# Identity product of the last tokens' second column piece moved behind the piece's first matmuls, and two VectorE steps moved behind the extra column

## The chip, the cores and the metric

The kernel runs on one core of a Trainium2 chip. The metric is device time in microseconds from one launch of the whole program; lower is better. Engines are called TensorE (PE in the rows), VectorE (DVE), ScalarE (ACT), GpSimd (POOL) and SyncE (SP). A "q" behind an engine's name marks its instruction queue, which issues transfers (DMAs).

## The reference

One layer of a hybrid encoder block over 512 tokens of width 1024. Only its last lines matter here: the feed-forward part's down projection is added to the residual stream, and each token's row of 1024 numbers is then divided by its root mean square and multiplied by a gain.

```python
def rms_norm(x, g):
    y = x * lax.rsqrt(jnp.mean(x * x, axis=-1, keepdims=True) + EPS)
    return y * g

def conv_glu_ffn(h, w_up, w_conv, b_conv, w_down):
    a, u = jnp.split(h @ w_up, 2, axis=-1)
    return (jax.nn.gelu(dwconv3(a, w_conv, b_conv)) * u) @ w_down

    x = x + merged @ w_out[l]
    x = x + conv_glu_ffn(rms_norm(x, ffn_norm_g[l]), w_ffn_up[l], ...)
return rms_norm(x, final_norm_g)
```

A token's norm needs the sum of squares over its whole row, so nothing of a row can be written out before its last column is known.

## The kernel before

All matrix products run in a split form. Each float32 operand is cut into a high part and a remainder, and one product becomes three matmuls (high x high, high x low, low x high). For the down projection these three are the lines of `tile_mm` (L1256, L1257, L1258). A matmul of 512 columns comes every 0.23 us there, one of 256 columns every 0.12 us.

The down projection is done as seven products of half-size blocks, in the manner of Winograd. The last of them is T4. It has 11 steps over the inner dimension; a step takes 128 rows of weights, which arrive by DMA in pairs (tile `wr`), are cut into `wh` and `wl` by ScalarE and VectorE (L242, L243), and for the last five steps are kept in three larger buffers (`u_8441`, `u_8442`, `u_8443` in the lists below).

The tokens lie in four blocks of 128, the output columns in two halves of 512. `cv(t, f)` is the residual sum, in SBUF, of token block `t` and column half `f`. T4 ends the columns of half 0 for the token blocks 2 and 3; everything else is complete before it. Its sums lie in PSUM:

- block 2, half 0 (`pa_[0]`, `at_6569` in the lists): all 11 steps, 512 columns.
- block 3, half 0 (`pa_[1]`, `at_6570`): the first six steps with 512 columns. The last five (`hold=5`) are held back until block 2 is done, and then run in two pieces of 256 columns (`ends=pieces`): columns `one_` go on in `pa_[1]`, columns `two_` go into another bank, `pl` (`at_8384`).

The residual of block 3 comes in through TensorE, by a product with the identity matrix in float32, which the trace shows as two passes. For the first piece that is `last_residual` (L1419). For the second piece it is `last_half`: VectorE first adds the six finished steps to the residual (L1423), and the identity product (L1424) then opens bank `pl` with that sum.

`product` runs over the pairs of steps. The dictionary `then` names other work that is issued behind a given pair's weights, so entry 3 of T4 stands behind the fourth pair; entries are closures over VectorE, ScalarE and GpSimd steps, among them `finish(t, ...)`, which scales and writes out token blocks 0 and 1. `tc.issue_after(x)` puts what is issued in its body behind instruction `x` in the order of issue. Each engine runs its own list strictly in order, and waits between engines are placed by the framework from the tiles that are read and written; it also keeps reads of one PSUM tile by two engines in their order of issue.

After T4, the tail of the kernel (L1433 to L1457) does the norm of blocks 2 and 3:

- VectorE adds block 2's sum to the residual (L1433), ScalarE squares and sums it (L1272), VectorE adds the other half's sum (L1287), GpSimd raises it to the power -1/2 (L1288, one column), ScalarE and VectorE scale the two halves (L1444, L1294 called from L1446), and SyncE writes the block out (L1447).
- Block 3's first piece is copied with the gain (`oa`, L1436, VectorE) and squared (L1272, ScalarE, straight out of PSUM). Its sum `v` (L1440) goes through a power (L1442, GpSimd) into an extra column of `pl`, which holds the square root of the sum so far (L1449, VectorE). ScalarE squares the second piece together with that column (L1451), so that its sum is the row's whole sum; a last power (L1452) gives the row's factor. ScalarE scales half 1 (L1453) and writes it out (L1454); VectorE scales the second and first pieces (L1455, L1456), and SyncE writes them (L1457).

Of the kernel before, what the change touches and what calls it, by code (L numbers as in the profile page):

```python
# [14 lines left out]
ALU = mybir.AluOpType  # L15
# [4 lines left out]
D = 1024  # L20
# [5 lines left out]
HF = FT // 2  # L26
HB = (HF + 1) // 2
Hf = S // 2
# [93 lines left out]
def hybrid_block(ctx, tc, xg, xT, memT, wflat, vecs, gbias, nabias, out):  # L122
    nc = tc.nc
    V, A, G, PE, SY = nc.vector, nc.scalar, nc.gpsimd, nc.tensor, nc.sync
# [16 lines left out]
    def unit(dt=F32):  # L141
        return up.tile([P, UNIT], dt, tag="unit", name=nm("u"))

    def scr(n=512):
        return sp.tile([P, S], F32, tag="scr", name=nm("s"))[:, :n]

    def tiny(n):
        return tp.tile([P, 32], F32, tag="tiny", name=nm("y"), bufs=12)[:, :n]

    def mmps():  # L150
        return mmp.tile([P, 512], F32, tag="mm", name=nm("mm"))

    def atps():
        return atp.tile([P, 512], F32, tag="at", name=nm("at"))
# [37 lines left out]
    st = {"raw": 0, "split": 0}  # L192
# [55 lines left out]
    def weights(key):  # L248

        i, _, n = BINDEX[key]  # L250
        while st["raw"] <= min(i + RAW_AHEAD, len(BLOCKS) - 1):
            emit_raw(st["raw"])
            st["raw"] += 1
        while st["split"] <= min(i + SPLIT_AHEAD, len(BLOCKS) - 1):
            emit_split(st["split"])
            st["split"] += 1
        return split.pop(i)
# [59 lines left out]
    ident = cp.tile([P, P], F32, name="ident")  # L317
# [132 lines left out]
    def flush():  # L450

        while late:
            late.pop(0)()
# [19 lines left out]
    for k in range(KT):  # L473
        if k % 2 == 0:
            ws = weights(("mlq", k // 2))
# [86 lines left out]
    for c in range(3):  # L562
        n, nk = TMC[c], TMK[c]
        pss = [(mmps if c % 2 else atps)() for _ in range(NT)]
        for h in range(KT // nk):
            ws = weights(("tm", c, h))
# [6 lines left out]
        for t in range(NT):  # L573
# [7 lines left out]
            if c > 0:  # L581
# [5 lines left out]
                for q in range(2):  # L587
                    V.scalar_tensor_tensor(nvv[:, q, 1:3, :], pv[:, q], rc[:, t:t + 1], nvv[:, q, 0:4:3, :].bitcast(F32),
                                           op0=ALU.mult, op1=ALU.subtract)
# [513 lines left out]
    for i in range(4):  # L1103
        ws = weights(("memv", i))
# [10 lines left out]
    for f in range(4):  # L1115
        ps = proj(("naq", f), XH, XL)
        V.tensor_tensor(nq[:, f * S:(f + 1) * S].rearrange("p (b r c) -> p b r c", r=ROWS, b=4), rv(ps), rv(rb),
                        op=ALU.mult)
# [15 lines left out]
    for br in range(3):  # L1134
# [19 lines left out]
        for fp in range(4):  # L1154
# [8 lines left out]
            ws = weights(("br", br, fp))  # L1163
# [49 lines left out]
    def cv(t, f):  # L1213
        o = t % 2 * D + f * S
        return C[t // 2][:, o:o + S]
# [9 lines left out]
    pieces = [("R", 4), ("H", 4), ("nab", 2), ("E", 1)]  # L1225
    r0 = [tp.tile([P, S], F32, tag=tag, name=nm("r"), **({} if n < 4 else {"bufs": 4})) for tag, k in pieces for n in [k] for _ in range(k)]
    one_, two_ = slice(0, Hf), slice(Hf, S)

    def parts():

        us = [unit(F32R) for _ in range(3)]
        at = lambda i: us[i // 8][:, i % 8 * Hf:(i % 8 + 1) * Hf]
        return [at(2 * k) for k in range(HF)], [at(2 * k + 1) for k in range(HF)], us

    def product(name, ab, banks, first, hold=0, then={}, ends=None):

        ah, al, _ = ab
        ws = []
        for i in range(HB):
            ws += weights(("dn", name, i))  # L1240
            if i == 0:
                flush()
            with tc.issue_after(st["lo"]), tc.issue_after(st["hi"]):
                for g in then.get(i, ()):
                    g()
            for k in range(2 * i, len(ws)):
                for t in range(2):
                    if k < HF - hold or t == 0:
                        tile_mm(ah[k], al[k], ws[k], banks[t], t, first and k == 0)
        for bank, c in ends or []:  # L1250
            for k in range(HF - hold, HF):
                tile_mm(ah[k], al[k], [w[:, c] for w in ws[k]], bank, 1, False)

    def tile_mm(ah, al, w, bank, t, start):
        ts = slice(t * P, (t + 1) * P)
        PE.matmul(bank, ah[:, ts], w[0], start=start, stop=False, skip_group_check=True)  # L1256
        PE.matmul(bank, ah[:, ts], w[1], start=False, stop=False, skip_group_check=True)  # L1257
        PE.matmul(bank, al[:, ts], w[0], start=False, stop=True, skip_group_check=True)  # L1258

    def gather(banks, a, f, op):  # L1260

# [5 lines left out]
    ss = [sv[:, 2 * t:2 * t + 2] for t in range(NT)]  # L1267
# [16 lines left out]
    def power(t, v, f):  # L1284

        col = tiny(1)
        V.tensor_tensor(col, ss[t][:, f:f + 1], v, op=ALU.add)  # L1287
        G.tensor_tensor(col, col, nhalf[:, :1], op=ALU.pow)  # L1288
        return col

    def scaled(t, f, col, dst=None):

        dst = cv(t, f) if dst is None else dst
        V.scalar_tensor_tensor(dst, cv(t, f), col, gfin[:, f * S:(f + 1) * S], op0=ALU.mult, op1=ALU.mult)  # L1294

    def finish(t, v):

        col = power(t, v, 1)
        for f in range(2):
            scaled(t, f, col)  # L1300
        SY.dma_start(out[t * P:(t + 1) * P, :], C[t // 2][:, t % 2 * D:(t % 2 + 1) * D])
# [17 lines left out]
    for hh in range(2):  # L1319
# [6 lines left out]
        for j in range(HF):  # L1326
            f = HF * hh + j
            if f == 0:
# [7 lines left out]
                k = KT - 1  # L1336
# [47 lines left out]
        if hh == 0:  # L1384
            pa_, pd = [atps() for _ in range(2)], [mmps() for _ in range(2)]
            product("B11", a11, pa_, True, then={0: [conved], 1: [gelu], 2: [gated]})
            product("T3", s3, pd, True, then={1: [lambda: gather(pa_, 0, 0, ALU.add)]})
            late.append(lambda b=pd: (gather(b, 1, 0, ALU.subtract), gather(b, 1, 1, ALU.add)))
    pd, pc = [mmps() for _ in range(2)], [atps() for _ in range(2)]
    s2, gfin = parts(), unit()  # L1390
    SY.dma_start(gfin[:, :D], gbias[16:].partition_broadcast(P))

    def wide_slices(ab, cols):
# [8 lines left out]
        return [lambda u=u: group(u, min(4, HF - 4 * u)) for u in range(3)]  # L1402

    product("B21", a12, pd, True, then={0: [conved], 1: [gelu], 2: [gated]})
    a22 = parts()
    product("T1", s1, pc, True, then=also(slices(s2, r0, one_, 0), 1, lambda: gather(pd, 0, 0, ALU.add)))
# [6 lines left out]
    vs = {}  # L1413

    pl = atps()
    pieces = ((pa_[1][:, one_], one_), (pl[:, :Hf], two_))
# [2 lines left out]
        PE.matmul(pieces[0][0], ident, cv(3, 0)[:, one_], start=False, stop=False, skip_group_check=True)  # L1419

    def last_half():
        c = cv(3, 0)[:, two_]
        V.tensor_tensor(c, c, pa_[1][:, two_], op=ALU.add)  # L1423
        PE.matmul(pieces[1][0], ident, c, start=True, stop=False, skip_group_check=True)  # L1424

    product("T4", a22, pa_, False, hold=5, ends=pieces, then={
        0: [lambda: vs.update({t: early(t, t // 2) for t in range(NT)})],
        1: [lambda: gather(pc, 0, 1, ALU.add), lambda: ready(1, 0, 1)],
        2: [last_residual, lambda: finish(0, vs[0])],
        3: [last_half, lambda: finish(1, vs[1])],  # L1430
        4: [lambda: V.tensor_tensor(cv(2, 1), cv(2, 1), gfin[:, S:D], op=ALU.mult),
            lambda: V.tensor_tensor(cv(3, 1), cv(3, 1), gfin[:, S:D], op=ALU.mult)]})
    V.tensor_tensor(cv(2, 0), cv(2, 0), pa_[0], op=ALU.add)  # L1433
    squares(cv(2, 0), 2, 0)
    oa, ob = scr(), scr()
    left = V.tensor_tensor(oa[:, one_], pa_[1][:, one_], gfin[:, one_], op=ALU.mult).ins  # L1436
    col2 = power(2, vs[2], 0)
    sqa = squares(pa_[1][:, one_], 3, 0)
    v = tiny(1)
    part = V.tensor_tensor(v, ss[3][:, 0:1], vs[3], op=ALU.add).ins  # L1440
    col = tiny(1)
    G.tensor_tensor(col, v, nhalf[:, :1], op=ALU.pow)  # L1442
    with tc.issue_after(sqa):
        A.activation(cv(2, 1), cv(2, 1), AF.Copy, scale=col2)  # L1444
    with tc.issue_after(part):
        scaled(2, 0, col2)  # L1446
    SY.dma_start(out[2 * P:3 * P, :], C[1][:, :D])  # L1447

    V.scalar_tensor_tensor(pl[:, Hf:Hf + 1], v, D ** 0.5, col, op0=ALU.mult, op1=ALU.mult)  # L1449
    v, sq, col = tiny(1), scr(), tiny(1)  # L1450
    A.activation(sq[:, :Hf + 1], pl[:, :Hf + 1], AF.Square, scale=D ** -0.5, accum_out=v)  # L1451
    G.tensor_tensor(col, v, nhalf[:, :1], op=ALU.pow)  # L1452
# [113 lines left out]
```

## Time and profile before

| | |
|---|---|
| median of 3 runs | 868.74 us (867.68, 868.74, 869.0) |
| the profiled execution's own time | 868.39 us |
| its span, first to last instruction | 866.3 us |
| mean granted TensorE clock in it | 0.998 |
| busy: TensorE, VectorE, ScalarE, GpSimd | 857.5, 630.6, 482.4, 165.8 us |

The profiled execution lies 0.35 us under the median of the three runs and inside their spread of 1.3 us. Times in rows count from the span's start. In a row of the timeline the columns are the start, the duration, the engine, the line, the operation, what is written from what, the number of instructions merged into the row, and in brackets how long the engine sat idle before and what ended that wait.

### The profile page before, as it was taken

The numbers are of one execution on the slowest core, as the hardware profiler recorded it, in microseconds if no ns is written. First come the engines' busy times: TensorE is split into PE (matmuls) and PEld (weight loads), VectorE is DVE, ScalarE is ACT, GpSimd is POOL, SyncE is SP. The second block draws the span as 40 slices with busy tenths as digits, with TensorE's granted clock in tenths as the row PEclk, the third lists the DMA queues.
The fourth block names the chain that finished last, engine by engine and source line by source line (L and its number), as shares of the span: only waits on it lengthen the run. The fifth ranks groups of instructions, "written<-read, shape, count | busy, mean of one in ns | idle before, by whom it ended". The sixth has DMA issues, their size and how long they took to land.

```text
span 866.3 us, 12252 instructions
## 1 busy us (share of the span) xinstructions
PE 857.5 (99%) x4192; PEld 724.0 (84%) x4192; DVE 630.6 (73%) x1269; ACT 482.4 (56%) x1026; POOL 165.8 (19%) x279
## 2 busy tenths in 40 slices
PE   9999999999999999999999999999999999999996
PEld 7898889988888888888888888888888888888885
DVE  7695687775567758898667558777766777788885
ACT  7364457654456648888644445444554444446763
POOL 0101100001113584600002003322100333320001
PEclk9999999999999999999999999999999999999999
DMA  8324643534395665543236965546547222326663
GB/s 278 100 74 136 196 133 120 176 105 134 122 230 127 203 149 145 160 135 119 98 110 184 327 190 131 176 146 182 146 158 210 82 98 98 98 81 214 183 205 132
DMA packets 42222, 131.93 MB, mean 152 GB/s; under 512 B 6376, under 2 KB 11496, under 8 KB 40560
## 3 DMA queue, kind: packets, MB, share of 16 engines
q1 hardware_dynamic: 32384, 101.37, 35.2%
q0 software_dynamic: 9344, 29.39, 14.0%
q8 instruction: 33, 0.54, 0.2%
q10 hardware_dynamic: 432, 0.39, 0.1%
q14 instruction: 29, 0.24, 0.1%
HBM read 126.91 MB, written 27.28 MB: 178 GB/s over the span
## 4 chain that ended last, share of the span: by engine, by line
PE 97%; DVE 1%; DMA 1%; issue 0%; POOL 0%; ACT 0%; POOLq 0%; DVEq 0%
PE mm L260 25%; PE mm L262 25%; PE mm L261 25%; PE at L1258 2%; PE at L1257 2%; PE at L1256 2%; PE at L261 2%; PE at L260 2%; PE at L262 2%; PE mm L1257 1%; PE mm L1256 1%; PE mm L1258 1%; PE at L934 1%; PE at L787 1%; PE at L915 1%; PE at L789 1%
## 5 line engine op out<-in xcount | busy, mean ns | idle before, releaser
L260 PE MATMUL mm<-u,wh 128*128 128x512 f32 (+1 forms) x907 | 354.2, 390 | 0.0
L262 PE MATMUL mm<-u,wl 128*128 128x512 f32 (+1 forms) x907 | 350.2, 386 | 0.0
L261 PE MATMUL mm<-u,wh 128*128 128x512 f32 (+1 forms) x907 | 349.8, 386 | 0.0
L242 ACT ACTIVATE wh<-wr 128x512 fp32r<-128x512 f32 (+2 forms) x328 | 203.1, 625 | 172.5 <-PE mm L261 108.1
L243 DVE TENSOR_TENSOR wl<-wr,wh 128x512 fp32r<-128x512 f32 (+2 forms) x330 | 236.2, 718 | 75.1 <-ACT wh L242 69.3
L262 PEld LDWEIGHTS mm<-u,wl 128*128 128x128 f32 x907 | 170.4, 188 | 34.6
L261 PEld LDWEIGHTS mm<-u,wh 128*128 128x128 f32 x907 | 170.7, 188 | 32.6
L260 PEld LDWEIGHTS mm<-u,wh 128*128 128x128 f32 x907 | 170.6, 188 | 32.5
L600 POOL DMA_DIRECT2D u<-nav_d x128 | 62.7, 528 | 28.8 <-PE at L934 14.9
L1359 POOL TENSOR_TENSOR s<-s,rb 128x512 f32<-128x512 f32 x18 | 29.6, 1645 | 113.0 <-DVE s L1358 106.1
L169 POOL COPY y<-wl 128x1 f32<-128x1 f32 x24 | 6.9, 289 | 223.8 <-DVE wl L243 223.7
L1256 PE MATMUL at<-wh,u 128*128 128x512 f32 x100 | 39.1, 391 | 0.0
L1258 PE MATMUL at<-wh,u 128*128 128x512 f32 x100 | 38.9, 389 | 0.0
L1257 PE MATMUL at<-wl,u 128*128 128x512 f32 x100 | 38.9, 389 | 0.0
L1305 ACT ACTIVATE u<-r 128x256 fp32r<-128x256 f32 x44 | 17.7, 414 | 36.7 <-DVE r L1370 23.0
L520 ACT ACTIVATE s<-pad,vec 128x512 f32<-128x512 f32 x30 | 24.3, 811 | 15.4 <-DVE pad L518 14.8
L521 DVE SCALAR_TENSOR_TENSOR s<-pad,vec,s 128x512 f32<-128x512 f32 x30 | 22.9, 762 | 5.3 <-ACT s L520 5.2
L1306 DVE TENSOR_TENSOR u<-r,u 128x256 fp32r<-128x256 f32 x44 | 20.5, 474 | 6.2 <-ACT u L1305 6.2
L1355 ACT ACTIVATE s<-s 128x512 f32<-128x512 f32 x22 | 13.9, 634 | 19.7 <-DVE s L522 19.6
L1358 DVE SCALAR_TENSOR_TENSOR s<-s,s 128x512 f32<-128x512 f32 x22 | 15.2, 691 | 12.6 <-ACT s L1357 12.6
L522 DVE SCALAR_TENSOR_TENSOR s<-pad,vec,s 128x512 f32<-128x512 f32 x30 | 22.5, 750 | 0.7
L1256 PEld LDWEIGHTS at<-wh,u 128*128 128x128 f32 x100 | 18.8, 188 | 3.9
(336 smaller groups left out, 1251.0 us busy)
## 6 DMA issues: line engine op xcount, KB each, us to landing
wr<-wflat SPq DMA_DIRECT2D x140, 512.0 KB, 3.4
wr<-wsum_T SPq DMA_DIRECT2D x20, 512.0 KB, 3.8
wsum_T<-wflat POOLq DMA_DIRECT2D x8, 1024.0 KB, 10.0
wsum_T<-wflat POOLq DMA_DIRECT2D x6, 768.0 KB, 7.5
nab<-nabias SPq DMA_DIRECT2D x16, 256.0 KB, 2.7
u<-nav_d POOLq DMA_DIRECT2D x128, 32.0 KB, 3.1
s<-xT SPq DMA_DIRECT2D x15, 256.0 KB, 4.7
nav_d<-nv POOLq DMA_DIRECT2D x8, 256.0 KB, 2.5
```

Source lines behind the costliest of these rows:

```text
L242: st["hi"] = A.activation(h[:, u:v], src, AF.Copy).ins
L243: st["lo"] = V.tensor_tensor(l[:, u:v], src, h[:, u:v].bitcast(F32), op=ALU.subtract).ins
L260: PE.matmul(ps, lh, rh, start=start, stop=False)
L261: PE.matmul(ps, lh, rl, start=False, stop=False)
L262: st["mm"] = PE.matmul(ps, ll, rh, start=False, stop=stop).ins
L520: A.activation(t1, pad[:, 0:512], AF.Identity, scale=vcol(w, i), bias=vcol(b, i))
L521: V.scalar_tensor_tensor(t1, pad[:, 1:513], vcol(w, n + i), t1, op0=ALU.mult, op1=ALU.add)
L600: G.dma_start(vw[r * 32:(r + 1) * 32, i * 256:(i + 1) * 256], nav_v[hf, r, CW[b]:CW[b] + 32, hp * 256:(hp + 1) * 256])
L1256: PE.matmul(bank, ah[:, ts], w[0], start=start, stop=False, skip_group_check=True)
L1257: PE.matmul(bank, ah[:, ts], w[1], start=False, stop=False, skip_group_check=True)
L1258: PE.matmul(bank, al[:, ts], w[0], start=False, stop=True, skip_group_check=True)
L1359: ve.tensor_tensor(c, c, rb2, op=ALU.mult)
```

## The change

Three things move; nothing is computed anew and the number of instructions of each engine stays.

1. The identity product of the second piece no longer opens bank `pl`. The piece's first held step opens it (`start` is set for it), and the identity product is issued behind that step's three matmuls. VectorE's addition that feeds it stays where it was, in entry 3.
2. The copy of the first piece with the gain (`oa`) moves from ahead of the second squares to behind the step that writes the extra column.
3. The VectorE scaling of block 2's half 0 (`scaled(2, 0, col2)`) moves from behind the sum `v` to behind that same step, after the copy.

```diff
-        for bank, c in ends or []:
+        for n, (bank, c) in enumerate(ends or []):
             for k in range(HF - hold, HF):
-                tile_mm(ah[k], al[k], [w[:, c] for w in ws[k]], bank, 1, False)
+                tile_mm(ah[k], al[k], [w[:, c] for w in ws[k]], bank, 1, n > 0 and k == HF - hold)
+                if n > 0 and k == HF - hold:
+                    with tc.issue_after(st["mm"]):
+                        last_half()
...
     def last_half():
-        c = cv(3, 0)[:, two_]
-        V.tensor_tensor(c, c, pa_[1][:, two_], op=ALU.add)
-        PE.matmul(pieces[1][0], ident, c, start=True, stop=False, skip_group_check=True)
+        PE.matmul(pieces[1][0], ident, cv(3, 0)[:, two_], start=False, stop=False, skip_group_check=True)
...
-        3: [last_half, lambda: finish(1, vs[1])],
+        3: [lambda: V.tensor_tensor(cv(3, 0)[:, two_], cv(3, 0)[:, two_], pa_[1][:, two_], op=ALU.add),
+            lambda: finish(1, vs[1])],
...
     oa, ob = scr(), scr()
-    left = V.tensor_tensor(oa[:, one_], pa_[1][:, one_], gfin[:, one_], op=ALU.mult).ins
     col2 = power(2, vs[2], 0)
     sqa = squares(pa_[1][:, one_], 3, 0)
     v = tiny(1)
-    part = V.tensor_tensor(v, ss[3][:, 0:1], vs[3], op=ALU.add).ins
+    V.tensor_tensor(v, ss[3][:, 0:1], vs[3], op=ALU.add)
     col = tiny(1)
     G.tensor_tensor(col, v, nhalf[:, :1], op=ALU.pow)
     with tc.issue_after(sqa):
         A.activation(cv(2, 1), cv(2, 1), AF.Copy, scale=col2)
-    with tc.issue_after(part):
+    rest = V.scalar_tensor_tensor(pl[:, Hf:Hf + 1], v, D ** 0.5, col, op0=ALU.mult, op1=ALU.mult).ins
+    with tc.issue_after(rest):
+        V.tensor_tensor(oa[:, one_], pa_[1][:, one_], gfin[:, one_], op=ALU.mult)
         scaled(2, 0, col2)
     SY.dma_start(out[2 * P:3 * P, :], C[1][:, :D])
-
-    V.scalar_tensor_tensor(pl[:, Hf:Hf + 1], v, D ** 0.5, col, op0=ALU.mult, op1=ALU.mult)
```

Lines behind the first edit carry numbers 1 to 3 higher in the changed kernel: the three matmuls become L1259 to L1261, the squares L1275, the scaling L1297, the first power L1443.

TensorE in the seventh to eleventh step of T4 for block 2 (`at_6569`), before. `u_5526` is the buffer that holds the residual of the blocks 2 and 3:

```order
L1256 MATMUL at_6569<-u_8441,u_7961 128x512
L1257 MATMUL at_6569<-u_8441,u_7961 128x512
L1424 MATMUL at_8384<-u_5526,ident 128x256 [waits DVE_49]
L1258 MATMUL at_6569<-u_8441,u_7961 128x512
L1256 MATMUL at_6569<-u_8442,u_7962 128x512 [waits Activation_49]
```

And TensorE at the passage from the first piece to the second, in the changed kernel:

```order
L1261 MATMUL at_6570<-u_8443,u_7962 128x256
L1259 MATMUL at_8384<-u_8441,u_7961 128x256
L1260 MATMUL at_8384<-u_8441,u_7961 128x256
L1261 MATMUL at_8384<-u_8441,u_7961 128x256
L1425 MATMUL at_8384<-u_5526,ident 128x256
L1259 MATMUL at_8384<-u_8441,u_7961 128x256
```

The identity product goes from within block 2's eighth step to behind the second piece's first three matmuls, 28 rows later, and carries no wait of its own there.

VectorE from block 2's addition to the end, before:

```order
L1433 TENSOR_TENSOR u_5526<-u_5526,at_6569 128x512 [waits PE_49]
L1287 TENSOR_TENSOR y_8534<-sv 128x1 [waits Activation_49]
L1436 TENSOR_TENSOR s_8531<-at_6570,u_7819 128x256 [waits PE_49]
L1440 TENSOR_TENSOR y_8539<-sv 128x1 [waits Activation_49]
L1294 SCALAR_TENSOR_TENSOR u_5526<-u_5526,y_8534,u_7819 128x512 [waits Pool_49]
L1449 SCALAR_TENSOR_TENSOR at_8384<-y_8539,y_8541 128x1 [waits PE_49,Pool_49]
L1455 SCALAR_TENSOR_TENSOR s_8531<-at_8384,y_8549,u_7819 128x256 [waits Pool_49]
L1456 TENSOR_SCALAR s_8531<-s_8531,y_8549 128x256
```

The same stretch of VectorE in the changed kernel:

```order
L1435 TENSOR_TENSOR u_5526<-u_5526,at_6569 128x512 [waits PE_49]
L1290 TENSOR_TENSOR y_8533<-sv 128x1 [waits Activation_49]
L1441 TENSOR_TENSOR y_8538<-sv 128x1 [waits Activation_49]
L1446 SCALAR_TENSOR_TENSOR at_8384<-y_8538,y_8540 128x1 [waits PE_49,Pool_49]
L1448 TENSOR_TENSOR s_8531<-at_6570,u_7819 128x256
L1297 SCALAR_TENSOR_TENSOR u_5526<-u_5526,y_8533,u_7819 128x512
L1456 SCALAR_TENSOR_TENSOR s_8531<-at_8384,y_8549,u_7819 128x256 [waits Pool_49]
L1457 TENSOR_SCALAR s_8531<-s_8531,y_8549 128x256 [waits DVE_49]
```

The copy (`s_8531<-at_6570`) and the scaling of block 2 (`u_5526<-u_5526,y_8533`) stand behind the extra column's step now; the sum (`y_8538<-sv`) and that step each come up.

ScalarE's two squares, before:

```order
L1272 ACTIVATE s_8529,sv<-u_5526 128x512 [waits DVE_49]
L1272 ACTIVATE s_8537,sv<-at_6570 128x256 [waits DVE_49]
L1444 ACTIVATE u_5526<-u_5526,y_8534 128x512 [waits Pool_49]
L1451 ACTIVATE s_8548,y_8547<-at_8384 128x257 [waits DVE_49]
L1453 ACTIVATE s_8532<-u_5526,y_8549 128x512 [waits Pool_49]
```

And in the changed kernel:

```order
L1275 ACTIVATE s_8529,sv<-u_5526 128x512 [waits DVE_49]
L1275 ACTIVATE s_8536,sv<-at_6570 128x256 [waits PE_49]
L1445 ACTIVATE u_5526<-u_5526,y_8533 128x512 [waits Pool_49]
L1452 ACTIVATE s_8548,y_8547<-at_8384 128x257 [waits DVE_49]
L1454 ACTIVATE s_8532<-u_5526,y_8549 128x512 [waits Pool_49]
```

The order is the same; the second squares wait for TensorE where they waited for VectorE. The lists of GpSimd and SyncE keep their order.

2 lines of the change are left out of this document (1 added, 1 removed).

## The prediction

> **What bounds the kernel now.** I read the chain of waits first, by engine, and then the last 15 us of it in order of time, engine by engine, because nothing ahead of T4's eighth step moves.
>
> ```profile
> PE 97%; DVE 1%; DMA 1%; issue 0%; POOL 0%; ACT 0%; POOLq 0%; DVEq 0%
> 851.31 0.39 PE L1257 MATMUL at<-u,u 128*128 128x512 f32 x1
> 853.11 0.70 PE L1424 MATMUL at<-u,ident 128*128 128x256 f32 x2 [1.42 <-DVE u L1423]
> 853.46 0.58 PE L1258 MATMUL at<-u,u 128*128 128x512 f32 x1
> 853.88 0.40 PE L1256 MATMUL at<-u,u 128*128 128x512 f32 x1
> 854.11 0.39 PE L1257 MATMUL at<-u,u 128*128 128x512 f32 x1
> ...
> 855.93 0.28 PE L1256 MATMUL at<-u,u 128*128 128x256 f32 x1
> ...
> 859.40 0.28 PE L1258 MATMUL at<-u,u 128*128 128x256 f32 x1
> ```
>
> TensorE carries 97% of the path, and here it stops once: the identity product waits 1.42 us for VectorE's addition, and everything queued behind it waits too. TensorE ends at 859.40 + 0.28 = 859.68; the span ends at 866.3, so 6.6 us of norm and writing follow. Who is last there is read from the other engines.
>
> ```profile
> 852.04 0.69 DVE L243 TENSOR_TENSOR u<-wr,u 128x512 fp32r<-128x512 f32 x1
> 852.64 0.41 DVE L1423 TENSOR_TENSOR u<-u,at 128x256 f32<-128x256 f32 x1
> 853.18 1.42 DVE L1294 SCALAR_TENSOR_TENSOR u<-u,y,u 128x512 f32<-128x512 f32 x2
> 854.51 0.69 DVE L1431 TENSOR_TENSOR u<-u,u 128x512 f32<-128x512 f32 x1
> 855.12 0.69 DVE L1432 TENSOR_TENSOR u<-u,u 128x512 f32<-128x512 f32 x1
> 856.13 0.69 DVE L1433 TENSOR_TENSOR u<-u,at 128x512 f32<-128x512 f32 x1 [0.33 <-PE at L1258]
> 857.61 0.16 DVE L1287 TENSOR_TENSOR y<-sv 128x1 f32<-128x1 f32 x1 [0.79 <-ACT s L1272]
> 857.92 0.42 DVE L1436 TENSOR_TENSOR s<-at,u 128x256 f32<-128x256 f32 x1 [0.15 <-PE at L1258]
> 858.89 0.16 DVE L1440 TENSOR_TENSOR y<-sv 128x1 f32<-128x1 f32 x1 [0.54 <-ACT s L1272]
> 858.97 0.74 DVE L1294 SCALAR_TENSOR_TENSOR u<-u,y,u 128x512 f32<-128x512 f32 x1
> 860.15 0.17 DVE L1449 SCALAR_TENSOR_TENSOR at<-y,y 128x1 f32<-128x1 f32 x1 [0.44 <-POOL y L1442]
> 861.49 0.48 DVE L1455 SCALAR_TENSOR_TENSOR s<-at,y,u 128x256 f32<-128x256 f32 x1 [1.17 <-POOL y L1452]
> ```
>
> ```profile
> 856.85 0.63 ACT L1272 ACTIVATE s<-u 128x512 f32<-128x512 f32 x1 [6.27 <-DVE u L1433]
> 858.38 0.38 ACT L1272 ACTIVATE s<-at 128x256 f32<-128x256 f32 x1 [0.81 <-DVE s L1436]
> 858.75 0.71 ACT L1444 ACTIVATE u<-u,y 128x512 f32<-128x512 f32 x1
> 860.35 0.39 ACT L1451 ACTIVATE s<-at 128x257 f32<-128x257 f32 x1 [0.89 <-DVE at L1449]
> ```
>
> ```profile
> 857.85 0.55 POOL L1288 TENSOR_TENSOR y<-y,nhalf 128x1 f32<-128x1 f32 x1 [4.70 <-DVE y L1287]
> 859.13 0.99 POOL L1442 TENSOR_TENSOR y<-y,nhalf 128x1 f32<-128x1 f32 x1 [0.73 <-DVE y L1440]
> 860.90 0.55 POOL L1452 TENSOR_TENSOR y<-y,nhalf 128x1 f32<-128x1 f32 x1 [0.79 <-ACT s L1451]
> ```
>
> The extra column (L1449) starts at 860.15 and was released by the power at 860.12, not by TensorE, which ended 0.44 us earlier. So the path from the first piece on is: copy (L1436), second squares, sum (L1440), power (L1442), extra column, last squares, last power, scaling, write. Two rows stand out. The second squares wait 0.81 us for the copy, which only reads the same bank. And the power took 0.99 us beside VectorE's scaling (858.97 to 859.71), which has two large inputs in SBUF, but 0.55 us when VectorE was idle or read PSUM (L1436). It ended 0.41 us after that scaling: it was held up until then.
>
> **TensorE.** Without the wait L1258 follows L1257 by a matmul's step (854.11 - 853.88 = 0.23) at 851.54, and the next L1256 comes at 851.77, against 853.88: all that follows is 2.11 us earlier. The new waits that the third weight buffer gets are met: its remainder (L243) is ready at 852.73, and TensorE needs it seven matmuls after 851.77, at 853.38. VectorE's addition, still at 852.64, ends at 853.05; the first piece, which now waits for it, begins at 855.93 - 2.11 = 853.82. So both waits cost nothing, with 0.6 us in hand or more. The identity product's own work, 853.88 - 853.11 - 0.23 = 0.54 us, is paid in the second piece: TensorE ends at 859.68 - 2.11 + 0.54 = 858.11. Between 256-column matmuls no row shows it. Its bounds are nothing, if it hides in the weight loads, and 0.54 + 0.70 if its whole row comes on top; that is an end between 857.6 and 858.8. I take the row's own 0.54, and only an end past 858.6 would matter, as the first power shows below.
>
> **VectorE takes over as the limit at block 2.** TensorE is done with block 2 some 2.11 us before 856.1, at 854.0. But VectorE's queue has not moved: L1431 and L1432 start 0.61 apart, so L1433 starts at 855.12 + 0.61 = 855.73 instead of 856.13. **Gain 0.40**, not 2.11. This is what was late next.
>
> **The second squares.** The first squares start 856.85 - 856.13 = 0.72 after L1433, at 856.45, and take 0.63. The second ones now wait for TensorE alone, whose first piece ends at 857.9 - 2.11 = 855.8, so they follow at 857.08, against 858.38: 1.30 earlier, **0.90 more**.
>
> **The first power.** The sum starts 0.51 after the second squares (858.89 - 858.38), at 857.59. Block 2's own power is in the way: its sum starts 0.76 after the first squares (857.61 - 856.85), at 857.21, and its power runs 0.24 later, 857.45 to 858.00. Does VectorE's small sum at 857.59, with both inputs in SBUF, wait for that power? These rows, of a place 135 us earlier, are the nearest:
>
> ```profile
> 722.11 0.74 POOL L1377 TENSOR_TENSOR r<-r,u 128x256 f32<-128x256 f32 x1 [0.80 <-DVE u L1370]
> 722.51 0.61 DVE L1306 TENSOR_TENSOR u<-u,u 128x256 fp32r<-128x256 f32 x1 [0.48 <-ACT u L1305]
> 723.80 0.80 POOL L1380 TENSOR_TENSOR u<-u,r 128x256 f32<-128x256 f32 x1
> 723.93 1.22 DVE L243 TENSOR_TENSOR wl<-wr,wh 128x512 fp32r<-128x512 f32 x1
> ```
>
> L243 began inside a GpSimd product and took 1.22 us, against 0.69 above: 0.53 of waiting. So VectorE is held up as well when it comes second. I take it that the sum waits: it ends near 858.02, the power starts 0.08 later (859.13 - 858.89 - 0.16) at 858.10 and takes 0.55, with nothing beside it, to 858.65. If it doesn't wait, the power only follows the other one, 858.00 to 858.55. From the sum's start to the power's end it took 860.12 - 858.89 = 1.23 and takes 1.06: **0.17 more**. The extra column starts at 858.68, 1.47 earlier; TensorE, done at 858.11, is in time by 0.5 us.
>
> The Trainium skill, page "SBUF — State Buffer", section "Who interferes with whom", says that a VectorE instruction with two SBUF inputs and a GpSimd instruction that reads SBUF exclude each other, whichever issued first going first, for the whole instruction. The long rows agree (0.99 against 0.55, 1.22 against 0.69); for a one-column sum against a power no row exists. By that rule the sum waits and the gain is the 1.19 below; without it, 1.29.
>
> **The last power gets the neighbour that the first one lost.** The last squares start 0.20 after the extra column, at 858.88; ScalarE's scaling (L1444) is put ahead of them at 858.03 and ends at 858.74, in time by 0.14. The last power starts 0.55 later, at 859.43. VectorE meanwhile does the copy from 858.76 (0.08 after the extra column, as 858.89 to 858.97) and, 0.35 later, the scaling, 859.11 to 859.85. The power arrives inside it and ends 0.41 after it, at 860.26, instead of 859.98. It took 0.55 and takes 0.83: **0.28 lost**. VectorE is free at 859.85, so the last scaling waits for the power only and starts at 860.30, against 861.49.
>
> The sum is 0.40 + 0.90 + 0.17 - 0.28: **1.19 us earlier**.
>
> **The writes.** Block 2's write is issued behind the moved scaling, the last two behind the last scaling.
>
> ```profile
> 859.78 0.33 SPq L1447 DMA_DIRECT2D out<-u  x1
> 862.26 0.33 SPq L1457 DMA_DIRECT2D out<-s  x1
> ...
> 860.50:862.00 1.50, 0.00 (x0) 0.00 (x0) 0.51 (x2) 0.84 (x3) 0.55 (x1) 1.00 0.84 350
> 862.00:863.00 1.00, 0.00 (x0) 0.00 (x0) 0.23 (x1) 0.21 (x1) 0.00 (x0) 0.81 0.00 0
> 863.00:864.75 1.75, 0.00 (x0) 0.00 (x0) 0.00 (x0) 0.00 (x0) 0.00 (x0) 0.50 0.77 300
> ```
>
> The last two numbers of a window are the DMA engines' busy share and GB/s. Block 2's write moves from 859.78 to 859.92 and fills the DMA engines for 0.84 x 1.50 = 1.26 us, from about 860.7 to 862.0. The last two, issued 1.19 earlier near 861.06, start moving about 0.8 us later, at 861.9. The idle microsecond between the two bursts is used up and they touch, at a cost between 0 and 0.1 us. I take 0, since the first burst is ending there.
>
> **Rivals.**
>
> A. The power and VectorE don't hold each other up in the new place. Against it: 0.99 against 0.55 in this tail. For it: the margins are 0.3 us in the last power. Without either wait the gain is 0.40 + 0.90 + 0.27 = 1.57.
>
> B. The whole of TensorE's 2.11 reaches the end, less the identity product's 0.54 where it counts: 1.6 to 2.1. It needs VectorE's addition (L1433) to start before 855.1, so another order of its queue, which the change does not give.
>
> C. Less arrives: the identity product stops TensorE in the second piece for the 1.42 us it waits now, so that TensorE ends at 859.5 and the extra column waits for it. Then the extra column is 0.6 earlier and the gain 0.3 to 0.6. Its input is ready at 853.05 and TensorE comes to it some 3 us later, so little speaks for it.
>
> D. Slower: the moved scaling makes block 2's write so late that the last two queue behind it. Fully in a row, the writes need 0.8 + 1.26 + 0.77 x 1.75 = 3.4 us from block 2's issue; the last bytes move until about 864.7 now, so it decides from an issue later than 861.3, 1.4 us after my 859.92. Both powers would have to go ahead of the scaling and the copy, 0.99 each: then the issue is at 861.9 and the end 0.6 us later than before, 869.0. Against it: the scaling starts 0.3 us ahead of the last power.
>
> **How the numbers follow.** The profiled execution took 868.39, of which 866.3 is the span; 868.39 - 1.19 = 867.20. The median of the three runs is 0.35 higher; the mean of all four executions is 868.45, and 868.45 - 1.19 = 867.26, so I predict 867.3. Chances: my sum, with or without the wait of VectorE's small sum (1.19 or 1.29), 0.66; A 0.13; B 0.05; C 0.12; D 0.04. The runs before spread by 0.7 to either side; A's 1.57 and C's 0.3 give 866.9 and 868.1, so with that spread 866.3 to 868.6 holds 8 in 10. A measurement of this kernel tells about 0.2%, 1.74 us, from no change. My sum lies under that by 0.5, A by 0.2, B mostly over it. With the runs' spread I give a sixth of my sum (0.11), two fifths of A (0.05) and most of B (0.04) to faster, D to slower: faster 0.20, same 0.76, slower 0.04.
>
> **What would show it.** In the changed profile: no idle time before the identity product, and TensorE's last matmul near 857.8; L1435 starting near 855.7 with no wait for TensorE; the second squares right behind the first, near 857.1; the first power 0.55 long, the last one about 0.83; the last two writes issued near 861.1. The prediction is wrong if L1435 is not what the first squares wait for, if the last power takes 0.55, or if the last writes land more than 2.8 us after their issue.

## The result: 867.07 us, and where the time came from

The changed kernel takes 867.07 us (median; 866.29 to 868.7) where the kernel before took 868.49 in the same comparison. The ratio is 0.9983 with an interval of [0.9976, 0.9989], so 1.5 us less (0.95 to 2.1): a gain that is resolved, and still under the 0.2% named in the prediction. The profiled execution took 866.8, its span 864.7. Of all times quoted here one stands far off: one of experiment 3's twelve was 1452.33 us, at a granted clock of 0.557 where every other run on record had 0.995 or more; its ratio leaves it out.

To compare two executions I count time from VectorE's addition of the residual to the second piece (L1423 before, L1431 after), an instruction that no edit moves. It starts at 852.64 before and at 852.25 after. These 0.39 us come from ahead of the change; over the twelve profiles of this study the same start lies anywhere from 851.50 to 852.82. From that start to the end of the span it is 13.61 before and 12.41 after: **1.20 us** belong to the change in these two executions.

TensorE of the changed kernel, where the identity product stood and where it stands now:

```profile
850.80 0.39 PE L1260 MATMUL at<-u,u 128*128 128x512 f32 x1
851.03 0.39 PE L1261 MATMUL at<-u,u 128*128 128x512 f32 x1
...
855.33 0.28 PE L1261 MATMUL at<-u,u 128*128 128x256 f32 x1
855.45 0.59 PE L1425 MATMUL at<-u,ident 128*128 128x256 f32 x2
855.69 0.47 PE L1259 MATMUL at<-u,u 128*128 128x256 f32 x1
856.00 0.28 PE L1260 MATMUL at<-u,u 128*128 128x256 f32 x1
...
857.19 0.28 PE L1261 MATMUL at<-u,u 128*128 128x256 f32 x1
```

No idle time is left ahead of the identity product. Its own work is 0.43 us: from its start at 855.45 to the next step's second matmul (L1260) at 856.00 it is 0.55, against the 0.12 that one matmul's step takes (855.33 to 855.45). The last matmul ends at 857.47.

VectorE from the addition to the end:

```profile
852.25 0.41 DVE L1431 TENSOR_TENSOR u<-u,at 128x256 f32<-128x256 f32 x1
...
854.72 0.69 DVE L1434 TENSOR_TENSOR u<-u,u 128x512 f32<-128x512 f32 x1
855.32 0.69 DVE L1435 TENSOR_TENSOR u<-u,at 128x512 f32<-128x512 f32 x1
856.80 0.16 DVE L1290 TENSOR_TENSOR y<-sv 128x1 f32<-128x1 f32 x1 [0.79 <-ACT s L1275]
857.16 0.16 DVE L1441 TENSOR_TENSOR y<-sv 128x1 f32<-128x1 f32 x1 [0.20 <-ACT s L1275]
858.14 0.17 DVE L1446 SCALAR_TENSOR_TENSOR at<-y,y 128x1 f32<-128x1 f32 x1 [0.82 <-POOL y L1443]
858.22 0.42 DVE L1448 TENSOR_TENSOR s<-at,u 128x256 f32<-128x256 f32 x1
858.55 0.74 DVE L1297 SCALAR_TENSOR_TENSOR u<-u,y,u 128x512 f32<-128x512 f32 x1
859.73 0.48 DVE L1456 SCALAR_TENSOR_TENSOR s<-at,y,u 128x256 f32<-128x256 f32 x1 [0.44 <-POOL y L1453]
```

Block 2's addition (L1435) now follows L1434 with no wait for TensorE: its own queue sets it. ScalarE's squares, and GpSimd's three powers:

```profile
856.04 0.63 ACT L1275 ACTIVATE s<-u 128x512 f32<-128x512 f32 x1 [5.85 <-DVE u L1435]
856.67 0.36 ACT L1275 ACTIVATE s<-at 128x256 f32<-128x256 f32 x1
858.34 0.39 ACT L1452 ACTIVATE s<-at 128x257 f32<-128x257 f32 x1
```

```profile
857.04 0.55 POOL L1291 TENSOR_TENSOR y<-y,nhalf 128x1 f32<-128x1 f32 x1 [4.28 <-DVE y L1290]
857.56 0.55 POOL L1443 TENSOR_TENSOR y<-y,nhalf 128x1 f32<-128x1 f32 x1
858.89 0.81 POOL L1453 TENSOR_TENSOR y<-y,nhalf 128x1 f32<-128x1 f32 x1 [0.79 <-ACT s L1452]
```

The second squares run right behind the first. The first power (L1443) takes 0.55 where it took 0.99, and the last one (L1453) takes 0.81 where it took 0.55: it began inside VectorE's scaling (858.55 to 859.29) and ended at 859.70, 0.41 after it. The writes:

```profile
859.37 0.33 SPq L1450 DMA_DIRECT2D out<-u  x1
860.51 0.33 SPq L1458 DMA_DIRECT2D out<-s  x1
...
860.10:861.60 1.50, 0.00 (x0) 0.00 (x0) 0.38 (x2) 0.36 (x1) 0.00 (x0) 0.94 0.91 367
861.60:863.35 1.75, 0.00 (x0) 0.00 (x0) 0.00 (x0) 0.00 (x0) 0.00 (x0) 0.50 0.72 284
```

The last two numbers of a window are again the DMA engines' busy share and GB/s. Between the two bursts there is no idle stretch any more. SyncE's wait for the last write passes 2.88 us after the last issue; before, it was 2.73.

Term by term, each as the difference of two starts counted from the common addition:

| step | predicted | measured |
|---|---|---|
| block 2's addition (3.49 to 3.07) | +0.40 | +0.41 |
| second squares (5.74 to 4.42), beyond that | +0.90 | +0.90 |
| extra column (7.51 to 5.89), beyond that | +0.17 | +0.30 |
| last scaling (8.84 to 7.48), beyond that | -0.28 | -0.26 |
| landing of the last writes | 0 | -0.15 |
| sum | 1.19 | 1.20 |

### The profile page after: what moved, and what is told of

Read it like the earlier page. It is cut to its first block, busy times and chain, and to the rows that moved or that the text cites. A ratio compares the mean times of both kernels' runs of the same rounds, so it can differ in the third digit from the quotient of the medians.

```text
span 864.7 us, 12252 instructions
## 1 busy us (share of the span) xinstructions
PE 856.7 (99%) x4192; PEld 723.7 (84%) x4192; DVE 630.3 (73%) x1269; ACT 482.1 (56%) x1026; POOL 165.7 (19%) x279
## 4 chain that ended last, share of the span: by engine, by line
PE 97%; DVE 1%; DMA 1%; POOL 0%; issue 0%; ACT 0%; POOLq 0%; DVEq 0%
PE mm L260 25%; PE mm L262 25%; PE mm L261 25%; PE at L1259 2%; PE at L1261 2%; PE at L1260 2%; PE at L261 2%; PE at L260 2%; PE at L262 2%; PE mm L1259 1%; PE mm L1261 1%; PE mm L1260 1%; PE at L934 1%; PE at L787 1%; PE at L915 1%; PE at L789 1%
## 5 line engine op out<-in xcount | busy, mean ns | idle before, releaser
L243 DVE TENSOR_TENSOR wl<-wr,wh 128x512 fp32r<-128x512 f32 (+2 forms) x330 | 236.2, 719 | 73.8 <-ACT wh L242 70.1
L1259 PE MATMUL at<-wh,u 128*128 128x512 f32 x100 | 39.1, 391 | 0.0
L1261 PE MATMUL at<-wh,u 128*128 128x512 f32 x100 | 38.9, 389 | 0.0
L1260 PE MATMUL at<-wl,u 128*128 128x512 f32 x100 | 38.9, 389 | 0.0
L1261 PEld LDWEIGHTS at<-wh,u 128*128 128x128 f32 x100 | 18.8, 188 | 3.9
```

The lines of the kernel that those rows point to most:

```text
L243: st["lo"] = V.tensor_tensor(l[:, u:v], src, h[:, u:v].bitcast(F32), op=ALU.subtract).ins
L1261: st["mm"] = PE.matmul(bank, al[:, ts], w[0], start=False, stop=True, skip_group_check=True).ins
```

## The experiments

All runs in one table. The tail is the time from the common addition to the end of the span in that kernel's profile; "TensorE" is the end of its last matmul on the same scale. The last column is what released the extra column's step. The rows come from several comparisons, in which the kernel before had medians of 868.16 to 868.49 us; across them the ratios are to be compared, not the medians.

| kernel | median us | ratio to before | tail | TensorE | extra column waits for |
|---|---|---|---|---|---|
| before | | | 13.61 | 7.04 | first power |
| changed kernel | 867.07 | 0.9983 [0.9976, 0.9989] | 12.41 | 5.22 | first power |
| the same, again | 867.0 | 0.9981 [0.9972, 0.9989] | 12.64 | 5.99 | TensorE |
| 1 identity product alone | 867.71 | 0.9991 [0.9982, 0.9999] | 12.96 | 5.22 | first power |
| 2 copy and scaling alone | 868.62 | 1.0004 [0.9996, 1.0013] | 13.70 | 7.06 | TensorE |
| 3 scaling behind the sum | 866.63 | 0.9981 [0.9973, 0.999] | 12.15 | 5.70 | VectorE's queue |
| 4 scaling ahead of the copy | 866.93 | 0.9981 [0.9972, 0.9989] | 12.09 | 5.19 | first power |
| 5 gain products behind the addition | 866.65 | 0.9975 [0.9964, 0.9985] | 11.90 | 5.27 | TensorE |
| 6 both 5 and 4 | 866.25 | 0.9968 [0.9957, 0.998] | 11.20 | 4.87 | first power |
| 6 again | 866.47 | 0.998 [0.9971, 0.9989] | 12.19 | 5.87 | TensorE |
| 7 residual added twice | 867.57 | 0.9988 [0.9979, 0.9997] | 13.05 | 6.42 | TensorE |
| 8 both 5 and 3 | 866.13 | 0.9976 [0.9968, 0.9985] | 11.83 | 5.58 | TensorE |

A tail says what a change to VectorE's chain is worth. Where TensorE releases the extra column, it also holds how far ahead of TensorE's end the addition happened to start, which differs from one execution to the next (5.22 and 5.99 us in the two profiles of the changed kernel).

The second run of the changed kernel was expected 1.2 to 1.5 us under the kernel before, with the last writes landing about 0.15 us later after their issue. Its median is 1.4 us lower, and the writes landed 0.17 us later (2.90 against 2.73).

**1. The identity product alone.** The moved identity product stays; copy and scaling stand where they were.

```diff
+    left = V.tensor_tensor(oa[:, one_], pa_[1][:, one_], gfin[:, one_], op=ALU.mult).ins
     col2 = power(2, vs[2], 0)
...
-    V.tensor_tensor(v, ss[3][:, 0:1], vs[3], op=ALU.add)
+    part = V.tensor_tensor(v, ss[3][:, 0:1], vs[3], op=ALU.add).ins
...
-    rest = V.scalar_tensor_tensor(pl[:, Hf:Hf + 1], v, D ** 0.5, col, op0=ALU.mult, op1=ALU.mult).ins
-    with tc.issue_after(rest):
-        V.tensor_tensor(oa[:, one_], pa_[1][:, one_], gfin[:, one_], op=ALU.mult)
+    with tc.issue_after(part):
         scaled(2, 0, col2)
...
+    V.scalar_tensor_tensor(pl[:, Hf:Hf + 1], v, D ** 0.5, col, op0=ALU.mult, op1=ALU.mult)
```

> Identity product moved, copy and scaling left where they stood before. My theory: TensorE is 2.1 us earlier, but VectorE's queue lets block 2's addition start only 0.4 us earlier, and the copy then still stands ahead of the second squares. Copy at 857.3 in the time of the profile before, second squares at 857.74 (0.64 us earlier), the first power held up by the scaling as before (about 0.99 us), the last one 0.55 us. Gain over the kernel before 0.6 us, time about 867.9. Rival (the removed TensorE wait is the whole gain): 1.4 us as in the changed kernel, 867.1. Rival (TensorE ends nothing here): 0.

```profile
856.65 0.42 DVE L1438 TENSOR_TENSOR s<-at,u 128x256 f32<-128x256 f32 x1
...
857.60 0.16 DVE L1442 TENSOR_TENSOR y<-sv 128x1 f32<-128x1 f32 x1 [0.54 <-ACT s L1275]
...
857.84 0.99 POOL L1444 TENSOR_TENSOR y<-y,nhalf 128x1 f32<-128x1 f32 x1 [0.48 <-DVE y L1442]
```

The tail is 0.65 shorter than before, and the first power takes 0.99 again. 0.41 of it is the addition; the rest comes from the copy (L1438), which no longer waits for TensorE but still stands ahead of the second squares.

**2. Copy and scaling alone.** The identity product goes back to its old place behind its addition; the tail is the changed one. The loop over the held steps and entry 3 go back as well; of the edit against the changed kernel only this part is shown.

```diff
...
     def last_half():
-        PE.matmul(pieces[1][0], ident, cv(3, 0)[:, two_], start=False, stop=False, skip_group_check=True)
+        c = cv(3, 0)[:, two_]
+        V.tensor_tensor(c, c, pa_[1][:, two_], op=ALU.add)
+        PE.matmul(pieces[1][0], ident, c, start=True, stop=False, skip_group_check=True)
...
```

> Copy and scaling behind the extra column, identity product left where it stood before. My theory: the second squares follow the first piece's end, 0.46 us earlier, and the first power takes 0.55 us, but now TensorE's end at 859.68 releases the extra column (0.43 us earlier instead of 0.9), and the last power is held up by the scaling, 0.26 us. Gain about 0.2 us over the kernel before, 868.3; so the two parts alone add up to 0.8 of the 1.4 us of both, since each uncovers the other's limit. Rival (the tail alone makes the gain): 1.0 us or more. Rival (the parts are independent): the gains of this run and of the identity product alone add up to 1.4 us.

```profile
852.91 0.70 PE L1424 MATMUL at<-u,ident 128*128 128x256 f32 x2 [0.87 <-DVE u L1423]
...
859.62 0.17 DVE L1444 SCALAR_TENSOR_TENSOR at<-y,y 128x1 f32<-128x1 f32 x1 [1.21 <-PE at L1258]
...
860.37 0.81 POOL L1451 TENSOR_TENSOR y<-y,nhalf 128x1 f32<-128x1 f32 x1 [1.33 <-ACT s L1450]
```

The tail is 0.08 longer, where a gain of 0.2 was expected. The extra column comes no earlier than TensorE's last matmul allows (7.06), so only 0.33 of what the squares and the first power give arrives; the held-up last power and the closer writes then take it back. Alone, the two parts give 0.65 and -0.08 in these profiles; together they give 1.20. The times go the same way: by the ratios 0.8 us less (0.1 to 1.6) and 0.3 more (0.3 less to 1.1 more) alone, 1.5 less together. Each uncovers what the other would otherwise run into.

**3. The scaling behind the sum again.** The changed kernel, with block 2's scaling back between the small sum and the extra column, and the copy left at its new place.

```diff
-    V.tensor_tensor(v, ss[3][:, 0:1], vs[3], op=ALU.add)
+    part = V.tensor_tensor(v, ss[3][:, 0:1], vs[3], op=ALU.add).ins
...
+    with tc.issue_after(part):
+        scaled(2, 0, col2)
...
     with tc.issue_after(rest):
         V.tensor_tensor(oa[:, one_], pa_[1][:, one_], gfin[:, one_], op=ALU.mult)
-        scaled(2, 0, col2)
```

> The changed kernel with block 2's scaling put back behind the sum (only the copy stays behind the extra column). In the time of the changed kernel's profile: the scaling can start at 857.62, inside the first power (857.56 to 858.10). If they hold each other up, either the scaling ends near 858.7 (it waits, over 1 us long) or the power near 858.8; the extra column comes 0.5 to 0.7 us later, the last power takes 0.55 instead of 0.81, net loss 0.25 to 0.45 us against the changed kernel, gain over the kernel before about 1.1. Rival (no mutual hold-up): scaling 0.74 us long, extra column 0.2 later, last power 0.55 (0.26 won): no loss or 0.1 us better than the changed kernel.

```profile
857.29 0.75 DVE L1297 SCALAR_TENSOR_TENSOR u<-u,y,u 128x512 f32<-128x512 f32 x1 [0.31 <-POOL y L1291]
857.96 0.16 DVE L1448 SCALAR_TENSOR_TENSOR at<-y,y 128x1 f32<-128x1 f32 x1
```

```profile
857.23 0.55 POOL L1443 TENSOR_TENSOR y<-y,nhalf 128x1 f32<-128x1 f32 x1
858.71 0.55 POOL L1454 TENSOR_TENSOR y<-y,nhalf 128x1 f32<-128x1 f32 x1 [0.93 <-ACT s L1453]
```

A miss: the tail is 0.26 shorter than the changed kernel's, not longer. The first power started at 857.23, the scaling 0.07 later, inside it; both kept their own length, 0.55 and 0.75. The scaling then costs the extra column 0.15 (6.04 against 5.89), and the last power, with nothing beside it, is 0.55. Block 2's write goes out 0.9 earlier and the last writes land 2.74 after their issue, as before the change. So the scaling need not have moved: once the second squares no longer wait for the copy, the first power begins ahead of the scaling and is not held up in the old place either. The times of 3 and of the changed kernel do not tell them apart.

**4. The scaling ahead of the copy.**

```diff
     with tc.issue_after(rest):
-        V.tensor_tensor(oa[:, one_], pa_[1][:, one_], gfin[:, one_], op=ALU.mult)
         scaled(2, 0, col2)
+        V.tensor_tensor(oa[:, one_], pa_[1][:, one_], gfin[:, one_], op=ALU.mult)
```

> The changed kernel with the scaling ahead of the copy (both behind the extra column). My theory (the scaling, with two inputs in SBUF, holds up the last power; the copy, which reads PSUM, does not): the scaling runs 858.22 to 858.96 in the time of the changed kernel's profile, is over as the last power arrives at 858.89, and the power takes about 0.55 to 0.6 instead of 0.81; block 2's write goes out 0.33 us earlier and touches the last two less. Gain 0.25 us in the chain plus up to 0.1 in the writes over the changed kernel, 1.6 to 1.8 over the kernel before. Rival (the power's length has another reason): 0.8 us as before, gain 0.

```profile
858.22 0.75 DVE L1297 SCALAR_TENSOR_TENSOR u<-u,y,u 128x512 f32<-128x512 f32 x1
858.89 0.42 DVE L1449 TENSOR_TENSOR s<-at,u 128x256 f32<-128x256 f32 x1
...
858.90 0.55 POOL L1453 TENSOR_TENSOR y<-y,nhalf 128x1 f32<-128x1 f32 x1 [0.79 <-ACT s L1452]
```

The last power starts at 858.90, near the end of the scaling (858.97), and takes 0.55; the last scaling is 0.26 earlier than in the changed kernel and the tail 0.32 shorter. That is the term of -0.26 in the table above, taken away. The times do not tell the two kernels apart (0.9981 and 0.9983 of the kernel before).

**5. VectorE's two gain products behind block 2's addition.** If VectorE's queue sets that addition, two products ahead of it, 0.6 each, are what to move.

```diff
-        4: [lambda: V.tensor_tensor(cv(2, 1), cv(2, 1), gfin[:, S:D], op=ALU.mult),
-            lambda: V.tensor_tensor(cv(3, 1), cv(3, 1), gfin[:, S:D], op=ALU.mult)]})
-    V.tensor_tensor(cv(2, 0), cv(2, 0), pa_[0], op=ALU.add)
+        })
+    add = V.tensor_tensor(cv(2, 0), cv(2, 0), pa_[0], op=ALU.add).ins
+    with tc.issue_after(add):
+        V.tensor_tensor(cv(2, 1), cv(2, 1), gfin[:, S:D], op=ALU.mult)
+        V.tensor_tensor(cv(3, 1), cv(3, 1), gfin[:, S:D], op=ALU.mult)
```

> The changed kernel with VectorE's two gain products put behind block 2's addition instead of ahead of it. My theory (VectorE's queue, not TensorE, now sets the addition): the addition starts 1.2 us earlier, at 854.1 in the time of the changed kernel's profile; the squares and the first power follow, until TensorE's last matmul (857.47) releases the extra column at 857.5 instead of 858.14. Gain over the changed kernel 0.6 us, about 2.0 over the kernel before. Rival (TensorE or ScalarE sets the tail): the same time as the changed kernel.

```profile
854.06 0.68 DVE L1434 TENSOR_TENSOR u<-u,at 128x512 f32<-128x512 f32 x1
...
857.58 0.17 DVE L1448 SCALAR_TENSOR_TENSOR at<-y,y 128x1 f32<-128x1 f32 x1 [1.49 <-PE at L1261]
```

The addition starts 1.87 after the common one instead of 3.07, 1.2 earlier, as the queue theory has it. Of that 0.50 reaches the extra column, since TensorE's last matmul (5.27) now releases it: the limit goes back to TensorE.

**6. Both 5 and 4**, run twice.

> The run before with the scaling ahead of the copy as well. If the two limits are independent, both gains add: 0.6 + 0.3 us over the changed kernel, about 2.3 us over the kernel before, with the last power at 0.55 to 0.6 us. If the writes or TensorE's end take over, less.

> The gain products behind block 2's addition and the scaling ahead of the copy once more, to see how far TensorE's end moves against VectorE from one execution to the next: from VectorE's addition to TensorE's last end it was 4.87 us in the first run, 5.2 to 6.0 in the others of this order. If it lies past 5.0 here, the extra column is released by TensorE and the time from the addition to the span's end is longer than the first run's 11.2 us by as much. Gain over the kernel before 2.2 to 2.8 us.

The extra column in the first run, and in the second:

```profile
857.82 0.17 DVE L1448 SCALAR_TENSOR_TENSOR at<-y,y 128x1 f32<-128x1 f32 x1 [1.11 <-POOL y L1445]
```

```profile
857.49 0.17 DVE L1448 SCALAR_TENSOR_TENSOR at<-y,y 128x1 f32<-128x1 f32 x1 [1.63 <-PE at L1261]
```

The same program, with tails of 11.20 and 12.19. In the first TensorE ended at 4.87, ahead of the power's end at 4.97; in the second at 5.87, and the extra column waited for it. So the tail is longer by the 1.0 us that TensorE's end lies further from the addition. The run is not: the second execution took 865.83 us, the first 866.15. TensorE ended at 857.68 and 857.37 from the span's start; what moved more is the addition, from 852.82 to 851.50.

**7. The residual of the last tokens added twice.** This doubles the identity product's work in its new place, to see whether TensorE has the half a microsecond in hand that the prediction gives it.

```diff
                         last_half()
+                        last_half()
```

> The changed kernel with the identity product of the second piece issued twice, one behind the other (so the residual is added twice in those 256 columns of the last 128 tokens). My theory: TensorE's end has 0.64 us in hand in the changed kernel's profile (857.47 against the power's end at 858.10), a second product costs 0.2 to 0.5 us, so the time stays that of the changed kernel within 0.1 us. Rival (the moved product's own work is on the path): 0.2 to 0.5 us slower than the changed kernel.

```profile
858.34 0.17 DVE L1447 SCALAR_TENSOR_TENSOR at<-y,y 128x1 f32<-128x1 f32 x1 [1.47 <-PE at L1262]
```

A miss: TensorE ended at 6.42 and the extra column waited for it. The tail is 0.42 longer than that of the changed kernel's second profile, where TensorE was already last; but the addition started 0.42 earlier here, TensorE ends at 858.22 in both, and both spans are 864.9, so the tails alone show nothing. TensorE's end keeps a fixed distance to the issue of T4's fifth weight transfer (the section on why the prediction was right has a table of it), so that is where to count from here. TensorE's end comes 15.06 us behind that issue here and 14.63 in that profile, and the span's end 21.69 and 21.28 behind it: of the second product's 0.43 us, 0.41 arrived. The median is 0.57 above that kernel's in the same comparison; the two intervals overlap, so the times only point the same way. The half microsecond in hand was true of some executions, not of the kernel.

**8. Both 5 and 3.**

> The changed kernel with the gain products behind block 2's addition and block 2's scaling back behind the sum, as before the change (only the copy stays behind the extra column). Theory after the runs so far: a power holds VectorE up no longer once it has started, so the scaling (0.75 us, begun 0.07 after the first power) costs the extra column at most 0.15 us, nothing where TensorE's end releases it; the last power stands alone at 0.55 us; block 2's write leaves nearly 2 us ahead of the last two, which land 2.74 us after their issue instead of 2.82. From the start of VectorE's addition of the finished steps to the span's end 11.1 to 11.6 us, by where TensorE's end falls (12.4 and 12.6 in the changed kernel, 13.6 before). Gain over the kernel before 2.2 to 2.8 us. Rival (the port is held by whichever began first, for its whole length): scaling over 1 us long or the first power near 1 us, extra column 0.5 later, gain under 2 us.

```profile
857.00 0.75 DVE L1297 SCALAR_TENSOR_TENSOR u<-u,y,u 128x512 f32<-128x512 f32 x1 [0.38 <-POOL y L1291]
858.22 0.17 DVE L1450 SCALAR_TENSOR_TENSOR at<-y,y 128x1 f32<-128x1 f32 x1 [0.46 <-PE at L1261]
...
858.97 0.55 POOL L1456 TENSOR_TENSOR y<-y,nhalf 128x1 f32<-128x1 f32 x1 [1.48 <-ACT s L1455]
```

The scaling is 0.75 and the last power 0.55, neither held up; TensorE (5.58) sets the extra column, so the tail is 11.83, longer than the 11.1 to 11.6 expected. The lowest medians of the study are those of 8 (866.13) and 6 (866.25 and 866.47). Their intervals overlap the changed kernel's. In the comparison that had both, though, nine of the changed kernel's eleven times lie above 866.57, the slowest of 6's six, so that step is probably real; 8 was not timed beside the changed kernel.

## Why the prediction was right, point by point

867.3 was predicted and 867.07 measured, inside the range, and the decisive reading held: of TensorE's 2.11 us VectorE's queue let 0.41 through. Experiment 5 shows this by moving that queue. Of the rivals, B needed the addition (L1435) before 855.1; it started at 855.32 in an execution that was 0.39 ahead, which is 855.71 on the prediction's scale. D needed a slower kernel. A and C are answered below.

- **TensorE.** The wait is gone, and the last matmul begins 0.6 earlier (857.19) than the 857.8 that was foretold; 0.39 of that is this execution's earlier start. The identity product's own work was 0.43, not 0.54. Rival C, a new stop in the second piece, did not occur: L1425 shows no wait.
- **Second squares.** 1.31 earlier in all, 1.30 worked out. Experiment 1, with the copy back ahead of them, has them at 5.07 instead of 4.42.
- **First power.** Right in length (0.55). The choice that failed is that the small sum waits for the running power: L1441 began at 857.16 inside L1291's power (857.04 to 857.59) and took its usual 0.16, so the power followed the other directly and the extra column came 1.62 earlier, not 1.47. The alternative of 1.29 in the prediction was the true one.
- **Last power.** Held up as worked out, 0.81 against 0.83, and experiment 4 removes the hold-up. So rival A is out for this power; for the small sum, which did not wait, it was right.
- **Writes.** This term was mis-sized. They were costed at 0 with a bound of 0.1, and took 0.15 more, past the 2.8 us from issue to landing that the prediction itself named as a sign of being wrong. With block 2's write issued 2.48 ahead of the last one they landed 2.73 after it; 1.95 ahead 2.74 (experiment 3); 1.22 ahead 2.81 to 2.82 (experiments 4 and 6); 1.14 ahead 2.88. The distance of 1.14 is the one the prediction worked out (859.92 and 861.06). It took block 2's burst to last 0.84 x 1.50 = 1.26 us, as if at full share; in the profile before, its packets run from 860.62 to 862.04, 1.42 us. So the two bursts overlapped, and the first packet of the last writes came 0.99 us after SyncE's last issue instead of 0.84. This error and the small sum's cancel by luck, which is why the sum agrees to 0.01.
- **TensorE's half microsecond in hand.** It held in the profiled execution (857.47 against the power's end at 858.10) and failed in another one of the same kernel:

```profile
858.33 0.17 DVE L1446 SCALAR_TENSOR_TENSOR at<-y,y 128x1 f32<-128x1 f32 x1 [1.03 <-PE at L1261]
```

There TensorE ended at 5.99 and not at 5.22, and the gain from the common addition was 0.98 instead of 1.20. The prediction read a margin from one execution as a property of the kernel.

What moves the margin can be read from the profiles. T4's weights come in six transfers (`wr<-wsum_T`), and the fifth is the one that counts:

| profile | fifth transfer, issue to landing | landing to VectorE's addition | issue to TensorE's end | addition to TensorE's end |
|---|---|---|---|---|
| changed kernel | 4.34 | 5.07 | 14.63 | 5.22 |
| the same, again | 4.22 | 4.43 | 14.63 | 5.99 |
| 6 both 5 and 4 | 5.40 | 4.43 | 14.70 | 4.87 |
| 6 again | 4.33 | 4.43 | 14.63 | 5.87 |

The last column is the third less the first two. TensorE never idles on this stretch, and its end lies 14.63 us behind that issue (14.70 once) in all nine profiles of kernels without the stop and with one identity product. So it is VectorE that moves. The transfer took 4.2 to 5.4 us, and from its landing to the addition it is 4.43 to 4.44 us in eight of the twelve profiles and 5.02 to 5.08 in four (before, the changed kernel's first, 1 and 4). In those four a power of an earlier token block began inside VectorE's L243 and took 1.09 us instead of 0.57; VectorE's next scaling waited for it. No run moved these steps, so this is read, not tested.

The rule quoted in the prediction from the Trainium skill, "SBUF — State Buffer", "Who interferes with whom", holds here for one-column powers in one direction: a power that arrives inside VectorE's scaling ended 0.41 us after it in each of seven profiles (before, the changed kernel twice, experiments 1, 2, 5 and 7). In experiments 4 and 6 it began only 0.07 us ahead of the scaling's end and took its usual 0.55. That the one that issues first holds the other up for its whole length is not borne out by a one-column power that came first: the scaling kept 0.75 (experiments 3 and 8) and the small sum 0.16. The measurement decides; the prediction's wait of the small sum was that rule applied where no row had shown it.

Two things stay open. The times fell by 1.5 (0.95 to 2.1), the profiles from the common addition on by 1.0 to 1.2; the rest is inside the interval or lies ahead of anything that moved, and no run separates these. And why the weight transfer takes 4.2 us in one execution and 5.4 in another, or why the earlier power meets L243 in some and not in others, was not found. In the kernel before, the stop at the identity product hid all this: the waits were 1.42 and 0.87 (experiment 2, same place), and TensorE still ended at 7.04 and 7.06.

## What to carry to other kernels

Taking away one engine's wait gives what the next queue allows, here 0.4 of 2.1 us, so follow the next engine's queue instruction by instruction before pricing the wait. Edits in one tail don't add: tested alone these gave 0.65 and -0.08, together 1.20, and an edit made for the old order (the moved scaling) can be of no use in the new one, or a small loss: 0.26 us in the profiles, which the times do not resolve. A margin between two engines that is read from one profile should be checked in a second one before anything is laid into it.

## What was not expected of the hardware

- A one-column GpSimd power and a long VectorE scaling on SBUF: what counts is which of them began first, not that they overlap. A power that began 0.16 to 0.34 us into the scaling took 0.81 to 0.99 us, and 0.55 when it began 0.07 us ahead of the scaling's end; with the scaling begun 0.07 us behind the power, the scaling took 0.75 and the power 0.55, both unheld.
- TensorE's last matmul, counted from VectorE's addition, came between 4.87 and 5.99 us in nine profiles of kernels without the stop and with the identity product once. TensorE's end itself lay between 857.2 and 858.2 in them, and the addition between 851.5 and 852.8. From the issue of T4's fifth weight transfer, TensorE's end came after 14.63 us in eight of the nine and 14.70 in one.
- Two writes of 256 KB issued 1.14 us behind one of 512 KB land 0.15 us later than with 2.48 us between; with 1.22 us it is 0.08 to 0.09, and with 1.95 us nothing is lost.
